# A hybrid encoder layer: two-block chunks in the opening, up rows a pair ahead, the down stage's memory in order of release, and the last norm with its products beside it

## The chip, the cores and the metric

The kernel runs on one core of one Trainium2 chip. The metric is the time of one execution on the device in microseconds. Before the change it is 1643.92 us, the median of three runs (1643.7 to 1643.96). A core has five engines with queues of their own, worked off in order: TensorE (PE in the profile; its weight loads are PEld), VectorE (DVE), ScalarE (ACT), GpSimd (POOL) and SyncE (SP, which here only issues transfers).

## The reference

One layer over 1024 prompt frames and 8 times 16 sample frames, 1152 rows of 1024 columns together:

```python
h = rmsnorm(x, g_pre_mix)
qa, ka, va, qb, kb, vb, ga, gb = project(h, w_in)          # one product, 1024 -> 4352 columns
oa = band_attention(qa, ka, va, bias_a, sink)              # own chunk and 2 before, 8 heads on 2
ob = band_attention(qb, kb, vb, bias_b, None)              # own chunk and 8 before, 8 heads
merged = sigmoid(ga) * (oa @ w_oa) + sigmoid(gb) * (ob @ w_ob)
x = x + rmsnorm(merged @ w_out, g_post_mix)
u, g = split(rmsnorm(x, g_pre_ffn) @ w_upg)                # 1024 -> 2 x 3072
c = conv_b + sum over tap of conv_w[tap] * upad[:, tap:tap + s]   # causal, width 3
x = x + rmsnorm((gelu(c) * g) @ w_down, g_post_ffn)
```

`rmsnorm(x, g)` is x divided by the root of its mean square over a row (plus 1e-6), times g. The new keys, values and convolution rows are returned too.

## The kernel before, in words

All products run on TensorE with factors split into a high and a low part, so that one product of a block is three matmuls (high by high, and the two mixed ones; `chunk_product`, L143). The big products (projection, up, down) use a scheme of Strassen and Winograd: the factors are cut in two by two quarters, seven products of quarters replace eight, and sums and differences of quarters (the forms) are made on VectorE and ScalarE beforehand. The rows are the columns of the right factor: half of the 1152, 576, go through two PSUM banks as two chunks of 288 columns (`CW`).

*Opening.* Nine blocks of 128 rows of x are fetched by SyncE. Class `Block` squares a block on ScalarE with a sum per row (L274), gets the root from VectorE (L96) and GpSimd (L97), multiplies by root and gain on VectorE (`norm`, L278), transposes it on TensorE (L286, eight transposes into two banks `tp`), and writes the high part on ScalarE (L302) and the low part on VectorE (L307) into the right factor `xk`. The gain is a row that one transfer spreads over 128 partitions (L79). Class `Away` (L222) holds the products of the first quarter alone for seven pairs of output tiles (`ixh`), which need no forms. They fill TensorE while the blocks come in: `run` makes twelve matmuls of one half and one chunk, `copy` brings the result from PSUM to `ia0h` or `ia1h` on ScalarE. The order of TensorE, ScalarE and VectorE in the opening is written out by hand (L316 on). Beside it run the position tables: a product `pe` (L392), a copy `ea`, and the store of `tab_a`.

*Projection.* `right_factors` makes the forms (`sums`, L408, and their high and low parts, L208 and L209, named `t`). For each pair of tiles, `head` and `tail` (L440, L456) run the products: first `iz` and `ix` with the forms, and last `iz` with `a_i`. `left_factors` makes forms of the weight tiles (L127 to L133) and splits them (L173, L174). `plus` adds a PSUM bank to a tile (L188).

*Up stage.* 24 pairs of tiles of the up weights; a tail multiplies, `take` copies PSUM out, then follow the convolution (L1195, L1197, L1199), the gate, and four stores of the result to DRAM (`z_dr`, L1217 to L1223). For the first pairs (`NH` = 5), part of the convolution's rows was put to DRAM earlier and comes back by three transfers (L1204, `w<-c_dr`). The tile `w` that they land in alternates between two (`r1[f % 2]`). After the last pair, the new convolution rows are stored (L1259).

*Down stage.* `raws` (L1288 on) fetches pairs of z tiles and down weights (names such as `z12r`, `wd12r`: one transfer for each of the two tiles, L1295 and L1296), `split` and `split_samples` make high and low parts, and TensorE multiplies into `p20s` and others (L1366), which are gathered in `yacc`. The tiles of this stage take the memory of the up stage's; where a tile lies decides which earlier instruction it must wait for, and with it the order in which SyncE's queue is filled. `finish` (L1404) makes the last norm of a block of rows: a square on ScalarE, scaling and power on GpSimd, then on VectorE the product with root and gain (L1419) and the sum with the residual (L1422), and the store. `start_finish` runs it in two steps, so that the second step of one block lies behind the products of the next.

Outside of the manual stretches a scheduler sets the order of each engine's instructions.

## Time and profile before

| | us |
|---|---|
| median of three runs | 1643.92 |
| profiled execution, its own time | 1648.29 |
| profiled execution, span | 1646.5 |
| TensorE busy | 1591.7 |
| VectorE busy | 1096.0 |
| ScalarE busy | 726.1 |
| GpSimd busy | 215.9 |
| mean granted clock of TensorE | 0.992 of full |

The span is the time between the first and the last recorded instruction; the execution's own time holds a little more around it. Busy time is the sum over the whole span; it does not say whether an engine's idle time matters. That is read from the waits: an idle stretch ends when something else has finished, and the profile names that something behind an arrow. A granted clock of 1.00 is TensorE's level of 2.4 GHz, 0.50 that of 1.2 GHz, and a value between them is a mixture within the stretch.

### The profile page before, as it was taken

Reading aid. Unit: us, or ns where it says so; the run is one execution under the profiler, and the core shown is the slowest. Engines: PE = TensorE matmul, PEld = TensorE weight load, DVE = VectorE, ACT = ScalarE, POOL = GpSimd, SP = SyncE. Lnnn points to the kernel's source line nnn. Section 1 sums busy time; section 2 is a strip of 40 time slices with the busy share of each in tenths; the row PEclk is TensorE's granted clock in tenths of the full one; section 3 lists DMA queues with packets and bytes.
Section 4 is the critical chain, followed back from the end, with each engine's and each line's share of the span. In section 5 each row is a group of like instructions: output and inputs, shape, how many; then the busy total and the mean of one; then the engine's idle time right before and its main releaser. Section 6 shows DMA issues by size and latency. Waiting matters only on the chain. (4 is left out here: it accounts for less than half of the span.)

```text
span 1646.5 us, 27860 instructions
## 1 busy us (share of the span) xinstructions
PE 1591.7 (97%) x10887; PEld 1471.5 (89%) x10887; DVE 1096.0 (67%) x2015; ACT 726.1 (44%) x1411; POOL 215.9 (13%) x293
## 2 busy tenths in 40 slices
PE   6999999999999999999999999999999998999997
PEld 5999999878788889978799999999999997888886
DVE  6965544677777746353597866667666665966986
ACT  7611233566555544332373344444444444534342
POOL 1000000221110004310002311122111110000004
PEclk9999999999999999999999999999999999999999
DMA  7743321664543155342164312212212228053023
GB/s 257 250 166 136 119 95 73 215 183 146 167 152 102 60 198 183 120 166 90 67 205 139 106 66 81 69 67 81 81 66 81 75 80 314 1 215 110 1 100 130
DMA packets 93636, 206.47 MB, mean 125 GB/s; under 512 B 19464, under 2 KB 43320, under 8 KB 93504
## 3 DMA queue, kind: packets, MB, share of 16 engines
q1 hardware_dynamic: 93504, 204.69, 36.4%
q8 instruction: 85, 1.39, 0.3%
q14 instruction: 47, 0.39, 0.1%
HBM read 148.13 MB, written 61.24 MB: 127 GB/s over the span
## 5 line engine op out<-in xcount | busy, mean ns | idle before, releaser
L143 PE MATMUL x<-xot,s 128*128 128x288 f32 x1152 | 157.7, 295 | 1.5 <-DVE w L1156 1.5
L143 PEld LDWEIGHTS x<-xot,s 128*128 128x128 f32 x1152 | 154.9, 188 | 1.7 <-ACT a L1019 1.7
L1366 PE MATMUL x<-wbp,zap 128*128 128x512 f32 x576 | 135.3, 389 | 0.0
L1366 PEld LDWEIGHTS x<-wbp,zap 128*128 128x128 f32 x576 | 108.1, 188 | 22.5
L1366 PE MATMUL p<-wbp,zap 128*128 128x512 f32 x432 | 102.4, 394 | 0.0
L1019 ACT ACTIVATE s<-uw 128x512 fp32r<-128x512 f32 x96 | 60.1, 627 | 94.6 <-issue 42.0
L671 ACT ACTIVATE p<-p,m 128x256 f32<-128x256 f32 (+4 forms) x128 | 74.8, 586 | 56.5 <-DVE m L666 56.5
L1366 PEld LDWEIGHTS p<-wbp,zap 128*128 128x128 f32 x432 | 82.4, 191 | 17.3
L1020 DVE TENSOR_TENSOR s<-uw,s 128x512 fp32r<-128x512 f32 x96 | 70.1, 730 | 34.0 <-ACT s L1019 34.0
L1197 DVE SCALAR_TENSOR_TENSOR wk<-w,cw,wk 128x128 f32<-128x128 f32 (+2 forms) x144 | 83.2, 614 | 7.4 <-ACT wk L1195 6.6
L1020 DVE TENSOR_TENSOR a<-uw,a 128x512 fp32r<-128x512 f32 x62 | 42.9, 693 | 63.3 <-ACT a L1019 62.0
L143 PE MATMUL x<-xob,s 128*128 128x288 f32 x576 | 81.1, 295 | 3.2 <-ACT wk L1195 1.4
L143 PEld LDWEIGHTS x<-xob,s 128*128 128x128 f32 x576 | 78.1, 188 | 3.8 <-ACT wk L1195 1.6
L143 PE MATMUL z<-xot,s 128*128 128x288 f32 x576 | 80.7, 295 | 0.0
L143 PE MATMUL z<-xot,a 128*128 128x288 f32 x576 | 80.7, 295 | 0.0
L143 PE MATMUL ix<-t,s_i 128*128 128x288 f32 x576 | 78.6, 295 | 0.3 <-DVE iu L188 0.3
L143 PEld LDWEIGHTS z<-xot,s 128*128 128x128 f32 x576 | 78.1, 188 | 0.0
L143 PEld LDWEIGHTS z<-xot,a 128*128 128x128 f32 x576 | 78.1, 188 | 0.0
L143 PEld LDWEIGHTS ix<-t,s_i 128*128 128x128 f32 x576 | 77.2, 188 | 0.5 <-issue 0.5
L173 ACT ACTIVATE s_i<-iw 128x512 fp32r<-128x512 f32 x48 | 30.3, 630 | 88.4 <-PE ix L143 49.0
L143 PE MATMUL x<-xob,a 128*128 128x288 f32 x456 | 63.9, 295 | 0.0
L143 PE MATMUL y<-xob,a 128*128 128x288 f32 x456 | 63.9, 295 | 0.0
(625 smaller groups left out, 3828.2 us busy)
## 6 DMA issues: line engine op xcount, KB each, us to landing
uw<-in_w_upg SPq DMA_DIRECT2D x53, 512.0 KB, 4.4
iw<-in_w_in SPq DMA_DIRECT2D x31, 512.0 KB, 4.6
gg<-in_dr SPq DMA_DIRECT2D x16, 576.0 KB, 3.7
z_dr<-wk SPq DMA_DIRECT2D x24, 256.0 KB, 2.1
in_dr<-gt SPq DMA_DIRECT2D x30, 192.0 KB, 1.9
z_dr<-wk SPq DMA_DIRECT2D x24, 224.0 KB, 1.9
xt<-in_x SPq DMA_DIRECT2D x9, 512.0 KB, 10.1
oT<-o_dr SPq DMA_DIRECT2D x8, 576.0 KB, 5.3
```

The source lines that it names most:

```text
L143: nc.tensor.matmul(ps, w[:, i, k], right(j, c, k), start=first and n == 0, stop=last and n == len(todo) - 1, skip_group_check=True)
L173: nc.scalar.activation(sp[:, 0], src, AF.Copy)
L671: nc.scalar.activation(p[h][:, 0:n], p[h][:, 0:n], AF.Exp, bias=least[h], scale=-1.0, accum_out=st.d[:, h, i:i + 1])
L1019: nc.scalar.activation(sp[:, 0], src, AF.Copy)
L1020: nc.vector.tensor_tensor(sp[:, 1], src, fr(sp[:, 0]), op=ALU.subtract)
L1197: nc.vector.scalar_tensor_tensor(out, src(t), cw[:, f, t:t + 1], out, op0=ALU.mult, op1=ALU.add)
L1366: nc.tensor.matmul(ps, z[:, i, k, c], w[:, j, k], start=first and n == 0, stop=last and n == 2, skip_group_check=True)
```

## The change

In the projection, the two chunks of 576 columns are 256 and 320 wide instead of 288 and 288, so that the first chunk of the first products is two blocks of rows. The gain of the first norm comes as one row of 4 KB on ScalarE's queue and is spread over the partitions by two matmuls with a column of ones; the first two blocks read it from PSUM, the others from a copy. The rows of weights for `Away` are packed two to a buffer. The up rows of a pair are asked for during the pair before. In the down stage the order of the memory pools changes, the stores of the last pair and of the convolution rows move to GpSimd's queue, and the gain of the last norm is fetched later. In the last norm the product with the gain is made apart, in halves and beside the square; the scaling is on VectorE; root and residual are applied in one instruction.

```diff
+    widths = (2 * P, 2 * CW - 2 * P)
     def chunk(c):
-        return slice(c * CW, (c + 1) * CW)
+        return slice(c * widths[0], widths[0] + c * widths[1])
...
+        def away_weights(f):
+            if f not in wraws:
+                box = wraw.tile([P, 2, KD, P], F32, name=f"iwh{f}", tag="uw")
+                for i in range(2 - (f + 1 == NA)):
+                    nc.sync.dma_start(box[:, i], w_in[pairs[f + i][0]])
+                    wraws[f + i] = box[:, i]
+            return wraws[f]
...
+            g1 = xs.tile([1, D], F32, name="g1")
+            nc.scalar.dma_start(g1[:], g_pre_mix[None, :])
+            ones = xs.tile([1, P], F32, name="ones")
+            nc.vector.memset(ones[:], 1.0)
+            gps = [psx.tile([P, 512], F32, name=f"gps{i}", tag="ps") for i in range(2)]
+            for i in range(2):
+                nc.tensor.matmul(gps[i][:], ones[:], g1[:, i * 512:(i + 1) * 512], start=True, stop=True)
+            gp = xs.tile([P, D], F32, name="gp")
...
-                if tb == 0:
-                    gp = bcast_row(xs, g_pre_mix, D, "gp")
...
                 def norm(self):
+                    if self.tb < 2:
+                        for i in range(2):
+                            c = slice(i * 512, (i + 1) * 512)
+                            nc.vector.scalar_tensor_tensor(self.xn[:, c], xts[self.tb][:, c], self.st[:, 1:2], gps[i][:],
+                                                           op0=ALU.mult, op1=ALU.mult)
+                        return
...
+        def up_rows(f):
+            if f not in got:
+                w = r1[f % 2].tile([P, 4 * 3 * 256], F32, name=f"w{f}", tag="act")
...
+                if f < NH:
+                    for dst, c, cols, samples in rows(u, us):
+                        nc.sync.dma_start(dst, by_sample(c_dr[f][:, c, cols], samples))
+                got[f] = w, u, us
+            return got[f]
...
-            w = r1[f % 2].tile([P, 4 * 3 * 256], F32, name=f"w{f}", tag="act")
+            w, u, us = up_rows(f)
+            if f + 1 < NH:
+                up_rows(f + 1)
...
-            nc.sync.dma_start(z_dr[f][:, H1:512], c2[:, 0:512 - H1])
+            queue = nc.gpsimd if f == NF - 1 else nc.sync
+            queue.dma_start(z_dr[f][:, H1:512], c2[:, 0:512 - H1])
...
-        nc.sync.dma_start(conv_new, cnew)
+        nc.gpsimd.dma_start(conv_new, cnew)
...
-        for q in range(3):
-            zp[q], wp[q] = right(f"zp{q}"), right(f"wp{q}")
+        def split_pools(q):
             za.append(right(f"za{q}"))
             wb.append(right(f"wb{q}"))
-            if q == 0:
-                yacc = right("yacc").tile([P, NT, 2, 512], F32, name="yacc")
+        split_pools(0)
+        zp[0], wp[0] = right("zp0"), right("wp0")
+        split_pools(1)
+        for q in (1, 2):
+            zp[q], wp[q] = right(f"zp{q}"), right(f"wp{q}")
+        split_pools(2)
         zsp = [right(f"zs{i}") for i in range(6)]
         for q in range(3, 6):
             zp[q], wp[q] = right(f"zp{q}"), right(f"wp{q}")
+        yacc = right("yacc").tile([P, NT, 2, 512], F32, name="yacc")
...
-            rstd_of(st[:, 0:1], st[:, 2:3], nc.gpsimd)
+            last = n == NT - 1
+            for i in range(2):
+                c = slice(i * 512, (i + 1) * 512)
+                if i:
+                    yield
+                    nc.vector.tensor_scalar(st[:, 0:1], st[:, 0:1], 1.0 / D, EPS, op0=ALU.mult, op1=ALU.add)
+                nc.vector.tensor_tensor(yg[:, c], yt[:, c], gpo[:, c], op=ALU.mult)
+                sq = bank(psv, f"sq{tb}{i}")
+                nc.scalar.activation(sq, yt[:, c], AF.Square, accum_out=st[:, i:i + 1])
+            nc.vector.tensor_scalar(st[:, 2:3], st[:, 1:2], 1.0 / D, st[:, 0:1], op0=ALU.mult, op1=ALU.add)
+            nc.gpsimd.tensor_tensor(st[:, 2:3], st[:, 2:3], nhalf[:, 0:1], op=ALU.pow)
             yield
...
+            for c in [slice(0, 512), slice(512, D)] if last else [slice(0, D)]:
+                nc.vector.scalar_tensor_tensor(yt[:, c], yg[:, c], st[:, 2:3], x1[:, c], op0=ALU.mult, op1=ALU.add)
                 nc.sync.dma_start(y[tb][:, c], yt[:, c])
...
+        def start_finish(tb, products, add):
+            ends = finish(tb, box["n"])
+            next(ends)
             box["n"] += 1
+            products()
+            if box["n"] == NT:
+                next(pending.pop(), None)
+            add()
             next(ends)
```

TensorE's queue at the start of the program, before: `tp` are a block's transposes, `ixh_0` and `ixh_1` the two chunks of an `Away` product, `xk_128` and `xk_129` its two halves.

```order
L286 MATMUL tp_0_200<-ident,xn_190 128x128 x4
L286 MATMUL tp_1_205<-ident,xn_190 128x128 x4
L286 MATMUL tp_0_228<-ident,xn_196 128x128 x4
L286 MATMUL tp_1_233<-ident,xn_196 128x128 x4
L286 MATMUL tp_0_248<-ident,xn_224 128x128 x4
L286 MATMUL tp_1_253<-ident,xn_224 128x128 x4
L143 MATMUL ixh_0_268<-xk_128,ih_0_215 128x288 x12
L286 MATMUL tp_0_281<-ident,xn_244 128x128 x4
L286 MATMUL tp_1_286<-ident,xn_244 128x128 x4
L143 MATMUL ixh_0_268<-xk_129,ih_0_218 128x288 x12
```

The same place after the change (`gps` are the products that spread the gain):

```order
L274 MATMUL gps_167<-g_163,ones 128x512
L274 MATMUL gps_168<-g_163,ones 128x512
L314 MATMUL tp_0_207<-ident,xn_196 128x128 x4
L314 MATMUL tp_1_212<-ident,xn_196 128x128 x4
L314 MATMUL tp_0_233<-ident,xn_203 128x128 x4
L314 MATMUL tp_1_238<-ident,xn_203 128x128 x4
L143 MATMUL ixh_0_252<-xk_128,ih_0_225 128x256 x12
L314 MATMUL tp_0_280<-ident,xn_248 128x128 x4
L314 MATMUL tp_1_285<-ident,xn_248 128x128 x4
L143 MATMUL ixh_0_252<-xk_129,ih_0_228 128x256 x12
L143 MATMUL ixh_0_313<-xk_128,ih_1_267 128x256 x12
```

The first twelve matmuls stand behind the transposes of two blocks instead of three, and two products of the gain stand ahead of all.

VectorE's queue after the change, from the low parts of the last `Away` weights on; the first `sums` is the row that writes where the position tables' tiles lay.

```order
L177 TENSOR_TENSOR ih_4_692<-iwh_689,ih_4_692 128x512
L212 TENSOR_TENSOR xk_128<-b_148,xk_128 128x4x256
L212 TENSOR_TENSOR xk_128<-b_148,xk_128 128x4x320
L177 TENSOR_TENSOR ih_4_695<-iwh_689,ih_4_695 128x512
L438 TENSOR_TENSOR sums<-b_149,b_148 128x4x256
L438 TENSOR_TENSOR sums<-b_149,b_148 128x4x320
L212 TENSOR_TENSOR t_615<-sums,t_615 128x4x256
L177 TENSOR_TENSOR ih_5_756<-iwh_689,ih_5_756 128x512
```

The low parts of `xk` stand ahead of the first form now; all that follows stands behind it.

SyncE's queue at the start of the down stage, before:

```order
L1223 DMA z_dr_9204<-wk 128x128
L1475 DMA gpo<-in_g_post_ffn 128x1024
L1295 DMA z14r<-z_dr_9196 128x1152
L1296 DMA wd14r<-in_w_down 128x1024
L1295 DMA z14r<-z_dr_9197 128x1152
L1295 DMA z12r<-z_dr_9194 128x1152
L1296 DMA wd12r<-in_w_down 128x1024
L1295 DMA z12r<-z_dr_9195 128x1152
L1259 DMA out<-st 128x432
L1296 DMA wd12r<-in_w_down 128x1024
L1296 DMA wd14r<-in_w_down 128x1024
L1222 DMA z_dr_9205<-wk 128x448
```

After:

```order
L1266 DMA z_dr_9212<-wk 128x128
L1344 DMA z12r<-z_dr_9202 128x1152
L1345 DMA wd12r<-in_w_down 128x1024
L1344 DMA z12r<-z_dr_9203 128x1152
L1345 DMA wd12r<-in_w_down 128x1024
L1344 DMA z14r<-z_dr_9204 128x1152
L1345 DMA wd14r<-in_w_down 128x1024
L1344 DMA z14r<-z_dr_9205 128x1152
L1345 DMA wd14r<-in_w_down 128x1024
L1344 DMA z16r<-z_dr_9206 128x1152
```

The first pair's loads stand ahead of the second's and together, and the store of the convolution rows (`out<-st`) and the last pair's stores of z have left the queue.

## Rows read from the trace of the kernel before

**Rows 1.** The page, busy time, share of the span and instructions
```profile
PE 1591.7 (97%) x10887; PEld 1471.5 (89%) x10887; DVE 1096.0 (67%) x2015; ACT 726.1 (44%) x1411; POOL 215.9 (13%) x293
```

**Rows 2.** Table of waits, TensorE: waiter, releaser, us in total, times, longest
```profile
PE tp L286 <- DVE xn L278: 12.9, 5, 7.9
PE p20s L1366 <- ACT wbp L1304: 5.8, 1, 5.8
...
PE x L143 <- DVE w L1156: 1.5, 1, 1.5
...
PE x L143 <- DVE wk L1156: 0.5, 1, 0.5
```

**Rows 3.** Timeline, TensorE, opening: start us, length us, instruction, idle before
```profile
39.14 1.06 PE L286 MATMUL tp<-ident,xn 128*128 128x128 f32 x8 [0.18 <-DVE xn L278]
...
46.36 0.81 PE L392 MATMUL pe<-oh,tt 32*8 32x384 f32 x2
...
52.28 24.38 PE L143 MATMUL ixh<-xk,ih 128*128 128x288 f32 x168 [1.74 <-ACT ia0h L239]
76.50 3.34 PE L143 MATMUL iz<-t,s_i 128*128 128x288 f32 x24
79.68 3.35 PE L143 MATMUL ix<-t,s_i 128*128 128x288 f32 x24
```

**Rows 4.** Timeline, VectorE, opening
```profile
6.58 1.28 DVE L278 SCALAR_TENSOR_TENSOR xn<-xt,st,gp 128x1024 f32<-128x1024 f32 x1 [0.83 <-DMA gp<-in_g_pre_mix]
...
34.58 1.35 DVE L408 TENSOR_TENSOR sums<-b,b 128x1152 f32<-128x1152 f32 x1
35.85 0.15 DVE L96 TENSOR_SCALAR st<-st 128x1 f32<-128x1 f32 x1
...
74.66 1.29 DVE L174 TENSOR_TENSOR s_i<-iw,s_i 128x512 fp32r<-128x512 f32 x2
```

**Rows 5.** Timeline, ScalarE, opening
```profile
49.37 0.63 ACT L173 ACTIVATE ih<-iw 128x512 fp32r<-128x512 f32 x1 [2.25 <-DMA iw<-in_w_in]
```

**Rows 6.** The page, transfers: count, KB each, median us to landing
```profile
z_dr<-wk SPq DMA_DIRECT2D x24, 224.0 KB, 1.9
```

**Rows 7.** Timeline, SyncE's queue, start of the down stage
```profile
1363.77 0.34 SPq L1259 DMA_DIRECT2D out<-st  x1
1364.15 0.43 SPq L1296 DMA_DIRECT2D wd12r<-in_w_down  x1
```

**Rows 8.** Timeline, ScalarE, start of the down stage
```profile
1370.95 1.06 ACT L1304 ACTIVATE wbp<-wd12r 128x1024 fp32r<-128x1024 f32 x1 [2.22 <-DMA wd12r<-in_w_down]
```

**Rows 9.** Timeline, TensorE, start of the down stage
```profile
1372.06 0.80 PE L1366 MATMUL p20s<-wbp,zs 128*128 128x512 f32 x1 [5.82 <-ACT wbp L1304]
...
1381.31 0.84 PE L1366 MATMUL p20s<-wbp,zs 128*128 128x512 f32 x3
...
1394.91 0.84 PE L1366 MATMUL p10s<-wbp,zs 128*128 128x512 f32 x3
```

**Rows 10.** Windows: us, busy (count) by engine, granted clock, DMA share, GB/s
```profile
1372.00:1374.00 2.00, 1.94 (x5) 1.56 (x6) 1.96 (x2) 1.07 (x2) 0.00 (x0) 0.50 0.94 235
```

**Rows 11.** Timeline, all engines, end
```profile
1636.12 0.69 DVE L1378 TENSOR_TENSOR yacc<-yacc,x 128x512 f32<-128x512 f32 x1 [0.94 <-PE x L1366]
...
1636.84 0.63 ACT L1413 ACTIVATE sqf<-yacc 128x512 f32<-128x512 f32 x1 [2.16 <-DVE yacc L1378]
...
1638.14 1.17 POOL L96 TENSOR_SCALAR stf<-stf 128x1 f32<-128x1 f32 x1
...
1639.98 1.42 DVE L1419 SCALAR_TENSOR_TENSOR yacc<-yacc,stf,gpo 128x512 f32<-128x512 f32 x2 [0.72 <-POOL stf L97]
...
1641.43 1.63 DVE L1422 TENSOR_TENSOR yacc<-yacc,x1f 128x512 f32<-128x512 f32 x1
```

**Rows 12.** Groups: busy us, mean ns of one, idle before
```profile
L143 PEld LDWEIGHTS x<-xot,s 128*128 128x128 f32 x1152 | 154.9, 188 | 1.7 <-ACT a L1019 1.7
...
L720 PE MATMUL o<-pk,vs 128*64 128x256 f32 x192 | 24.3, 388 | 0.0
```

More of the change, by code (lines that the diff above doesn't have):

```diff
@@ L148, in product, with banks @@
             chunk_product(ps[c], w, right, c, first, last)
-    def banks(pool, name):
-        return [pool.tile([P, 512], F32, name=f"{name}_{c}", tag="ps")[:, 0:CW] for c in range(2)]
+    def banks(pool, name, widths=(CW, CW)):
+        return [pool.tile([P, 512], F32, name=f"{name}_{c}", tag="ps")[:, 0:n] for c, n in enumerate(widths)]
+    widths = (2 * P, 2 * CW - 2 * P)
     def chunk(c):
-        return slice(c * CW, (c + 1) * CW)
+        return slice(c * widths[0], widths[0] + c * widths[1])
     xkp = xk_stack.enter_context(tc.tile_pool(name="xk", bufs=1, reuse_waits="tile"))
@@ L187, in plus @@
             for c in range(2):
-                nc.vector.tensor_tensor(out[:, c], ps[c], t[:, c], op=ALU.add)
+                nc.vector.tensor_tensor(out[:, chunk(c)], ps[c], t[:, chunk(c)], op=ALU.add)
             return out
         def store(t, tile_no, half):
-            nc.sync.dma_start(in_dr[tile_no][:, half * 2 * CW:(half + 1) * 2 * CW], t[:].rearrange("p c n -> p (c n)"))
+            nc.sync.dma_start(in_dr[tile_no][:, half * 2 * CW:(half + 1) * 2 * CW], t[:])
         pairs = [(4, 5), (0, 1), (2, 3), (10, 14), (6, 7), (11, 15)] + [(18 + n, 26 + n) for n in range(6)]
         NA = 7
-        a1_dr = [dram.tile([P, 2, CW], F32, name=f"a1_dr{f}") for f in range(NA)]
+        a1_dr = [dram.tile([P, 2 * CW], F32, name=f"a1_dr{f}") for f in range(NA)]
         rf = {}
@@ L209, in parts_of, with weights @@
             nc.vector.tensor_tensor(lo, src, fr(hi), op=ALU.subtract)
-        def weights(f, n=2):
-            raw = wraw.tile([P, 2, KD, P], F32, name=f"iw{f}{n}", tag="uw")
-            for i in range(n):
+        def weights(f):
+            raw = wraw.tile([P, 2, KD, P], F32, name=f"iw{f}", tag="uw")
+            for i in range(2):
                 nc.sync.dma_start(raw[:, i], w_in[pairs[f][i]])
             return raw
+        def away_weights(f):
[5 more added lines that the diff above has]
+            return wraws[f]
         for i, name in enumerate(("b11", "b12")):
@@ L226, in __init__ @@
                 self.f, self.pool, self.early = f, pool, early
-                raw = wraws.pop(f, None) or weights(f, 1)
-                self.left = [split_left(raw[:, 0, 4 * i:4 * i + 4], f"ih1{i}_{f}") for i in range(2)]
+                raw = away_weights(f)
+                self.left = [split_left(raw[:, 4 * i:4 * i + 4], f"ih1{i}_{f}") for i in range(2)]
                 self.out = [two_chunks(f"ia{i}h{f}") for i in range(2)]
@@ L259, in encoder_step @@
                 xts.append(xt)
-                if tb == 0:
-                    gp = bcast_row(xs, g_pre_mix, D, "gp")
+                if tb == 1:
+                    box = wraw.tile([P, 2, KD, P], F32, name="iwh0", tag="uw")
                 if tb in (1, 3):
-                    wraws[tb // 2] = weights(tb // 2, 1)
+                    wraws[tb // 2] = box[:, tb // 2]
+                    nc.sync.dma_start(wraws[tb // 2], w_in[pairs[tb // 2][0]])
             class Block:
@@ L320, in encoder_step @@
                 b[0].transposed()
+                for i in range(2):
+                    nc.scalar.activation(gp[:, i * 512:(i + 1) * 512], gps[i][:], AF.Copy)
+                b[1].norm()
                 b[0].high()
-                b[1].norm()
                 b[0].low()
                 w0 = Away(0, psx, True)
-                enter()
                 b[1].transposed()
                 b[1].high()
+                b[1].low()
+                enter()
+                w0.run(0, 0)
                 b[2].norm()
-                b[1].low()
+                w0.copy(0, 0)
+                w1 = Away(1, psx, True)
                 enter()
@@ L453, in head_back @@
             nc.sync.dma_start(a[:], a1_dr[f][:])
-            return left_factors(weights(f), True, f"i{f}", split_left), banks(psx, f"ix{f}"), a
+            return left_factors(weights(f), True, f"i{f}", split_left), banks(psx, f"ix{f}", widths), a
         def tail(f, ops, xb, a, forms):
@@ L461, in tail @@
             t0, t1 = pairs[f]
-            zb = banks(psz, f"iz{f}")
+            zb = banks(psz, f"iz{f}", widths)
             product(zb, next(ops), of(rf["t3"]), True, False)
@@ L1200, in conv @@
                 return c
-            for dst, c, cols, samples in rows(u, us):
-                if yb is None:
-                    nc.sync.dma_start(dst, by_sample(c_dr[f][:, c, cols], samples))
-                else:
+            if yb is not None:
+                for dst, c, cols, samples in rows(u, us):
                     nc.vector.tensor_tensor(dst, by_sample(yb[c][:, cols], samples), by_sample(a[c][:, cols], samples),
```

83 lines of the change are left out of this document (33 added, 50 removed).

## The prediction, made before the changed kernel was run

> **What bounds the kernel now.** I read the busy line of the page first: TensorE is busy for 1591.7 us [rows 1] of a span of 1646.5, so the time is TensorE's work plus 54.8 us in which it has none. The table of TensorE's waits then says which of those gaps this change can reach [rows 2]: 12.9 us of transposes that wait for the first norms, 5.8 us at the start of the down stage, and four short waits of the up stage from 1.5 to 0.5 us (4.6 us together). The timelines of the engines in those places give the rest: what ended each wait, and what TensorE lost beside it. Behind the last products, which end just before the last add at 1636.12, comes a chain of small instructions on four engines [rows 11], and any microsecond taken from it counts in full. Elsewhere TensorE is dense, and only the pace of its matmuls could change anything.
>
> All sums are made against the profiled execution (1648.29 us, span 1646.5). The median of the runs shown is 1643.92, 4.4 us lower; I take the same difference from it.
>
> **Opening.** Three things change. The first norm no longer waits for a 512 KB broadcast of the gain (0.83 us idle ahead of it [rows 4]), which also stood ahead of the second block of x on SyncE's queue; the two one-row products that replace it need 4 KB and run before TensorE has anything else. The first product needs two blocks, not three. And weight rows two to five are asked for earlier. I walked the new orders of the engines with the durations of the trace: the transposes of the last block, at 39.14 before [rows 3], come out near 38.35, since blocks two to eight still cost one square, one power and one norm each. By then half a run of twelve matmuls more is done (0.7 us), so 1.5 us are gained there. Then the wait of 1.74 us ahead of 52.28 goes [rows 3]: ScalarE had waited 2.25 us for a weight row, until 49.37 [rows 5], and its copies that free TensorE's banks were queued behind. From 52.28 to 76.50 the 168 matmuls take 24.22 us, where at full clock 24 take 3.18 (76.50 to 79.68), 22.26 for 168 [rows 3]; the 1.96 us between is a lower clock after that wait, and goes with it. Together 1.5 + 1.74 + 1.96 = 5.2 us: the first tail starts near 71.3.
>
> What is late next is VectorE. In the new order nearly all of the Winograd forms stand behind one instruction, the first that writes the sums. Its memory is that of the position table's tiles, so it waits for the store of that table; before, the first form ran at 34.58 [rows 4]. The table's product, at 46.36 before [rows 3], comes 1.5 us earlier with the products around it: 44.9. Its own 0.8 us, ScalarE's copy of 0.5, which no longer stands behind a wait, and some 2.3 for issue and landing (1.9 us for a small store [rows 6]) make 48.5. Behind it on VectorE stand, up to the left factor of the tail's last product, twenty pieces of the forms' sums and low halves, at 256 or 320 columns and 1.27 us on average (34.58 to 35.85), thirteen 512-column steps of 0.60 us (two in 1.29, pipelined) [rows 4], and eight pieces of a quarter of that size, some 0.4 us by my estimate from these: 25.4 + 7.8 + 3.2 = 36.4 us. With 1 us for releases that is 85.9. TensorE, starting at 71.3, wants the factor four products of 3.2 us later, at 84.1, and I count 0.2 us more for an earlier piece. So about 2.0 us go back, while 0.3 us of a wait that the same place had before comes off: net 5.2 − 2.0 + 0.3 = 3.5 us. The two ends: 7.0 us if the forms aren't late and the earlier blocks gain more, and 1.0 us if the first form only starts at 51.
>
> **Chunk widths.** 2016 matmuls of the projection go from 288 columns to 1008 of 256 and 1008 of 320. At 288 one takes 3.18 / 24 = 132.5 ns [rows 3]; at 512, sixty take 13.60 us from 1381.31 to 1394.91, 226.7 ns each [rows 9]. The line through both is 0.42 ns a column, which gives 119.0 and 145.9, in sum 265 as before: nothing. From above, 256 columns cost the 126.6 ns of the attention's products of that shape (24.3 us over 192) [rows 12], 7.6 ns more than the line, 7.7 us lost over 1008; from below, the 132.5 ns scaled by columns (117.8) gives 1.2 us gained. The attention's products wait on copies between them, so I take the line: zero.
>
> **Up rows.** The code asks for the up rows one pair ahead, but the tile that they land in is one that the pair before last releases, and the new order of SyncE's queue has the fetches at the same places, behind the same stores. I price it at nothing, and expect the four waits [rows 2] again.
>
> **Start of the down stage.** Before, SyncE's queue held the store of the convolution state until 1363.77, and the second half of the first down weights only left behind it, at 1364.15 [rows 7]. ScalarE waited 2.22 us for that load until 1370.95 [rows 8], and TensorE 5.82 us, until 1372.06 [rows 9]. Then the clock: the 90 products from 1372.06 to 1394.91 took 22.85 us where six rounds of 3.40 are 20.40 [rows 9], so 2.45 us more, with a granted clock of 0.50 at first, the level of 1.2 GHz [rows 10]. Now the loads of the first pair lead the queue and the stores stand on GpSimd's. What the first load needs is memory that the last heads release before the stage; the four loads of the first pair, 2.2 MB, then have time to land. I take 5.82 + 2.45 = 8.27, less 0.4 for a first copy that still comes late: 7.9 us. The other end is 3, if a z tile of the first pairs comes as late as the last head allows.
>
> The new waits: copies into the output accumulator, on ScalarE and VectorE, now stand behind the stores of the last pair, which lie on its memory, and a later weight load behind the state's store. These copies come some 20 us into the stage. If such a store takes as long as the slowest load of this place (1364.15 to 1370.95, 6.8 us [rows 7, 8]), 10 us of cover are left; if the cover is gone, every microsecond counts, since products need the banks that these copies free. No transfer of before left GpSimd's queue, so its own landing time is not shown. The Trainium skill (SBUF — State Buffer, "SBUF: two separate sides") speaks against that queue: the descriptors of its transfers are written by GpSimd, and VectorE can lock it out while certain operations run; no row here shows it. By that rule the stores land late, and the sum would stay at 7.9 us up to a delay of 10 us, and lose one for one beyond it.
>
> **The end.** Before: the last add at 1636.12 (0.69), the square at 1636.84 (0.63) and its read, GpSimd's sum and its scaling at 1638.14 (1.17), its power, VectorE's two products from 1639.98 and its last add until 1643.06 [rows 11]. Now the scaling is one VectorE instruction (0.15 us as in the opening [rows 4]), and product and add are one instruction for each half, on a product made beside the square. The last add is held by the block before's final instruction, which is put ahead of it, by my walk until 1636.75. Then: add to 1637.45, square and read to 1638.3, scaling to 1638.5, power to 1639.1, two halves of 0.75 to 1640.6. That is 2.5 us gained; 3.2 if the add isn't held; 1.0 if the pieces wait on one another.
>
> **Sum.** 3.5 + 0 + 0 + 7.9 + 2.5 = 13.9 us: the profiled execution would be 1634.4, the median 1643.92 − 13.9 = 1630.0.
>
> **Rivals.** *VectorE eats the opening's gain*: the first form at 51 or later. For it speaks the long list behind that form; against it, that ScalarE's wait ahead of the table's copy goes. Opening 0, total 10.4: 1633.5. *The opening gives all*: the store lands early enough; opening 7.0, total 17.4: 1626.5. Against it stands the table's product, which TensorE still runs at its place among the others. *The down stage still waits*: its first loads are queued in front of one that waits for the last head, and 3 us come back; total 9.0: 1634.9. *The up rows do act*: 4.6 us more, 1625.4; the queue's unchanged order speaks against it, and then that part of the change would do what its code says.
>
> On the other side, *the 256-column matmul is paced by its weight load*: a load's record is 188 ns long beside every matmul [rows 12]. If at 256 columns it no longer fits, 1008 of them at 188 − 119 = 69 ns are 69 us lost: 1699. It decides from 13.9 us / 1008 = 13.8 ns on, 132.8 ns for a matmul of 256. Against it: at 288 columns matmuls follow each other every 132.5 ns with loads of that record, so the record is not the pace, and the attention's 256 run at 126.6.
>
> **How the numbers follow.** Forecast 0.54; opening eaten 0.19; opening all 0.11; down stage still waits 0.08; up rows act 0.03; weight-load pace 0.05. The forecast's own range is 1628 to 1632. All cases but the last two lie between 1626.5 and 1634.9; with part of the bound on the widths the range is 1625.5 to 1636. A measurement of this kernel tells 0.2%, 3.3 us, from no change. All cases but the last are faster by more than twice that; a part of the last (from 10.6 us of loss on) is no change, most of it slower: faster 0.94, same 0.02, slower 0.04.
>
> **What would show it.** In the changed kernel's timeline: the last block's transposes near 38.3; no wait near 50, the clock at full from 50 to 60; VectorE idle until about 48.5 ahead of its first sums, and TensorE waiting some 2 us for a left factor between 77 and 87; the four up-stage waits unchanged; the first product of the down stage within 0.5 us of the last of the up stage, at the level of 2.4 GHz; VectorE's scaling of 0.15 us and an end 4.5 us behind TensorE's last matmul. The forecast is wrong if 256 and 320 columns differ in sum from 265 ns, or if the loads of the down stage collide with the stores of the last pairs.

## The result, and the profile after

The changed kernel takes 1631.77 us (median of four runs, 1631.33 to 1635.94) against 1643.94 for the kernel before; the ratio is 0.9928, with a 95% interval from 0.9909 to 0.9947. The forecast was 1630.0, and the time lies 0.2 us inside the end of the forecast's own range (1628 to 1632). Six more runs of the changed kernel (e9 below) have a median of 1633.07, beside 1645.54 for the kernel before: the gain repeats, 12.2 and 12.5 us. Its profiled execution took 1635.94 us, with a span of 1634.1, against 1648.29 and 1646.5: 12.4 us less in both measures, where the sum had 13.9.

Where they came from is seen by cutting both traces at the same instructions of TensorE and comparing the lengths. The boundaries are the starts of: the first `iz` product, the end of the projection (its last product), the first transpose `pt` and the first product `mp`, the first `xh`, the last product of the up stage, the first `p20s`, the first `p10s`, then the end of the last matmul and of the span. The last column is a second trace of the changed kernel, from the experiments. Each column is one execution; what other traces of the same code have in these stretches is told with the experiments, and it matters for the opening and for the start of the down stage.

| stretch, us | before | changed | gained | changed again |
|---|---|---|---|---|
| opening, to the first tail | 76.50 | 71.89 | 4.61 | 72.35 |
| projection | 223.39 | 224.23 | −0.84 | 223.30 |
| on to the attentions | 8.12 | 8.25 | −0.13 | 8.68 |
| attentions | 295.72 | 296.81 | −1.09 | 297.75 |
| gates, output, norms | 215.34 | 216.14 | −0.80 | 214.22 |
| up stage | 546.88 | 547.27 | −0.39 | 547.13 |
| last up product to first down product | 6.11 | 0.13 | 5.98 | 0.13 |
| first six rounds of the down stage | 22.85 | 20.45 | 2.40 | 20.45 |
| rest of the down stage | 241.17 | 241.14 | 0.03 | 241.18 |
| behind TensorE's last matmul | 10.41 | 7.78 | 2.63 | 7.77 |

The opening on TensorE in the changed kernel (columns as in the timelines before):

```profile
36.52 1.06 PE L314 MATMUL tp<-ident,xn 128*128 128x128 f32 x8 [0.57 <-ACT ih L176]
...
68.61 3.44 PE L143 MATMUL ixh<-xk,ih 128*128 128x256 f32 x24 [2.24 <-ACT ia0h L251]
71.89 3.33 PE L143 MATMUL iz<-t,s_i 128*128 128x256 f32 x24
...
86.32 2.91 PE L143 MATMUL iz<-t,a_i 128*128 128x256 f32 x20 [0.92 <-DVE a_i L177]
...
97.65 2.03 PE L143 MATMUL ix<-t,s_i 128*128 128x320 f32 x12 [0.66 <-DVE iu L191]
```

The last transposes come at 36.52 instead of 39.14, and the wait at 52.28 of [rows 3] is gone. But a new one of 2.24 us, for the same kind of copy, stands at 68.61, and two of 0.92 and 0.66 us in the tails (in the second trace 1.48 us at 69.07, 0.90 in the tails, and nothing for the last). Behind the first of these stand VectorE, ScalarE and SyncE's queue, in this order:

```profile
47.62 2.63 DVE L438 TENSOR_TENSOR sums<-b,b 128x1024 f32<-128x1024 f32 x2 [1.61 <-DMA tab_a<-ea]
...
63.75 0.69 DVE L127 TENSOR_TENSOR iw<-iw 128x512 f32<-128x512 f32 x1 [2.35 <-DMA iw<-in_w_in]
```

```profile
67.01 1.27 ACT L211 ACTIVATE t<-sums 128x1280 fp32r<-128x1280 f32 x1 [1.53 <-DVE sums L438]
68.19 0.69 ACT L251 ACTIVATE ia0h<-ixh 128x256 f32<-128x256 f32 x2
```

```profile
47.51 4.96 SPq L92 DMA_DIRECT2D ext_a<-tab_a  x8
...
54.18 0.32 SPq L255 DMA_DIRECT2D a_dr<-ia0h  x1
54.59 1.70 SPq L217 DMA_DIRECT2D iw<-in_w_in  x2
```

VectorE's first `sums` waits for the table's store until 47.62 (34.58 in [rows 4]). Later VectorE stands 2.35 us, until 63.75, for the first pair of whole weights, whose load left at 54.59: behind eight transfers of the table that held SyncE's queue for 5 us, and directly behind a store of `Away` results that waits for ScalarE's copy. ScalarE's copy of a form waits for the `sums` behind it, and the copies `ia0h`, which free TensorE's banks, stand behind that one.

The start of the down stage, on TensorE and on SyncE's queue:

```profile
1364.72 0.87 PE L1415 MATMUL p20s<-wbp,zs 128*128 128x512 f32 x3
...
1385.17 0.84 PE L1415 MATMUL p10s<-wbp,zs 128*128 128x512 f32 x3
```

```profile
1348.01 0.40 SPq L1344 DMA_DIRECT2D z12r<-z_dr  x1
...
1350.49 0.43 SPq L1345 DMA_DIRECT2D wd12r<-in_w_down  x1
```

The loads of the first pair leave together, the second half of the weights at 1350.49, where [rows 7] has it at 1364.15. The first product follows the last head with no wait, and the 90 products take 20.45 us, the full clock's pace, against 22.85 in [rows 9]. The first copy into the accumulator, on ScalarE, and the largest store of the last pair, now on GpSimd's queue (the fence of transfers gives KB and us to landing):

```profile
1382.70 0.60 ACT L1425 ACTIVATE yacc<-p20s 128x512 f32<-128x512 f32 x1 [0.74 <-PE p20s L1415]
```

```profile
z_dr<-wk POOLq DMA_DIRECT2D x1, 256.0 KB, 6.1
```

The copy is released by its product, not by the stores: the last of them landed by 1376, over 6 us earlier. The end, all engines:

```profile
1625.80 1.28 DVE L1474 SCALAR_TENSOR_TENSOR yacc<-ygf,stf,x1f 128x1024 f32<-128x1024 f32 x1
1627.00 0.68 DVE L1427 TENSOR_TENSOR yacc<-yacc,x 128x512 f32<-128x512 f32 x1
...
1628.47 0.21 DVE L1470 TENSOR_SCALAR stf<-stf 128x1 f32<-128x1 f32 x1
...
1629.41 1.42 DVE L1474 SCALAR_TENSOR_TENSOR yacc<-ygf,stf,x1f 128x512 f32<-128x512 f32 x2 [0.73 <-POOL stf L1471]
```

The last add stands behind the block before's final instruction, which begins at 1625.80, and starts at 1627.00; VectorE's scaling takes 0.21 us where GpSimd's took 1.17 [rows 11]. The four waits of the up stage are still there, 4.8 us in all (4.7 before):

```profile
PE x L143 <- DVE wk L1200: 3.3, 3, 1.4
PE x L143 <- DVE w L1200: 1.5, 1, 1.5
```

### The profile page after: what moved, and what is told of

The parts are those of the page before. It is cut to its first block, busy times and chain, and to the rows that moved or that the text cites. A ratio compares the mean times of both kernels' runs of the same rounds, so it can differ in the third digit from the quotient of the medians.

```text
span 1634.1 us, 27922 instructions
## 1 busy us (share of the span) xinstructions
PE 1593.4 (98%) x10891; PEld 1470.7 (90%) x10891; DVE 1099.4 (67%) x2045; ACT 728.7 (45%) x1429; POOL 212.1 (13%) x287
## 4 chain that ended last, share of the span: by engine, by line
PE 86%; DVE 5%; ACT 3%; DMA 3%; issue 2%; POOL 1%; SPq 0%; DVEq 0%; POOLq 0%; ACTq 0%
PE x L143 16%; PE z L143 8%; PE x L1415 8%; PE ix L143 7%; PE p L1415 6%; PE iz L143 4%; PE y L143 4%; PE o L750 2%; PE d L117 2%; PE pt L735 2%; PE d L119 2%; PE r L1090 2%; PE mp L956 2%; PE mp L958 2%; PE mp L957 2%; PE d L118 2%
## 5 line engine op out<-in xcount | busy, mean ns | idle before, releaser
L143 PE MATMUL ix<-t,s_i 128*128 128x256 f32 (+1 forms) x576 | 78.4, 294 | 0.7 <-DVE iu L191 0.7
```

The costliest lines, as they stand in the source:

```text
L143: nc.tensor.matmul(ps, w[:, i, k], right(j, c, k), start=first and n == 0, stop=last and n == len(todo) - 1, skip_group_check=True)
```

## The experiments

Ten kernels were run. Their times scatter by some 3 us about the median between executions of one program, in part for the reason that run e9 shows, so where a stage is asked for, its length in the trace decides.

**The gain's row elsewhere (e1).** The forms were late because the opening's pool had grown by 4.6 KB a partition, and the sums came to lie on the table's tiles. Here the two new tiles go to other pools:

```diff
-            g1 = xs.tile([1, D], F32, name="g1")
+            g1 = wop.tile([1, D], F32, name="g1", tag="wop")
...
-            ones = xs.tile([1, P], F32, name="ones")
+            ones = pa.tile([1, P], F32, name="ones", tag="a")
```

> The changed kernel, with the gain's row and the column of ones put into the pools of the weight parts and copies, so that the opening's own pool is as small as in the kernel before and the forms' sums no longer lie on the position table's tiles. Theory 1 (VectorE's forms are late because of that overlap, and TensorE's waits of 2.24 us at 68.6, 0.92 at 86.3 and 0.66 at 97.7 come from it): the first form near 34, all three waits gone, 3.0 to 3.8 us less than the changed kernel's 1631.8, about 1628.3. Rival (the first pair of whole weights lands late at 63.7 whatever VectorE does, and holds it): the waits stay within 1 us, no more than 1 us gained.

Measured: 1633.54 us (1632.30 to 1635.36, six runs), ratio to before 0.9933 (0.9916 to 0.9950). VectorE and TensorE in its trace:

```profile
35.55 1.22 DVE L438 TENSOR_TENSOR sums<-b,xk 128x1024 f32<-128x1024 f32 x1
...
64.19 0.69 DVE L127 TENSOR_TENSOR iw<-iw 128x512 f32<-128x512 f32 x1 [2.84 <-DMA iw<-in_w_in]
```

```profile
38.65 1.07 PE L314 MATMUL tp<-ident,xn 128*128 128x128 f32 x8 [0.99 <-DVE xn L306]
...
68.87 3.44 PE L143 MATMUL ixh<-xk,ih 128*128 128x256 f32 x24 [1.67 <-ACT ia0h L251]
...
78.93 3.74 PE L143 MATMUL ix<-t,s_i 128*128 128x256 f32 x24 [0.28 <-DVE iu L191]
```

The first sums run at 34.35, as expected, and the second, shown here, at 35.55. Three traces have the changed kernel's opening unaltered: its own, that of e9 and that of e8. All three have a wait of 0.90 to 0.92 us for a left factor in the first tail, and it is gone here; one of 0.28 us stands at another place. The projection takes 222.83 us, against 224.23, 223.30 and 223.29 in the three. But the wait at 68 stays: 1.67 us here and 1.76 in e10, which has the same edit, against 2.24, 1.48 and 1.24; and VectorE still stands for the weights until 64.19. So theory 1 holds for the tails and the rival for the first wait. The last transposes, too, are later (38.65), since two forms now run ahead of the last norm on VectorE. Net, from the start to the end of the projection, 294.97 against 296.12, 295.65 and 295.70: 0.7 to 1.2 us, not 3 or more, and nothing that shows in the median.

**The sums in another slot (e2).** The order of VectorE's queue stays, only what the first form waits for changes:

```diff
-        tpool = [ph.enter_context(tc.tile_pool(name=f"t{i}", bufs=1, reuse_waits="tile")) for i in (3, 2, 1, 4)]
+        t3p, t2p, t4p, t1p = [ph.enter_context(tc.tile_pool(name=f"t{i}", bufs=1, reuse_waits="tile")) for i in (3, 2, 4, 1)]
+        tpool = [t3p, t2p, t1p, t4p]
```

> The changed kernel with the memory of the sums and of one form exchanged: the first form still stands at the same place of VectorE's queue but waits for the table's product and not for the store of the table. Theory 1a (the wait of 1.6 us for the store is what costs): the first form at 46.0 instead of 47.6, and 1.6 us of TensorE's 3.8 us of waits gone, 1630.2. Theory 1b (it is the place in the order, behind the low parts of four other pieces, that costs, not the wait): less than 0.7 us gained, 1631.1 to 1632.

Measured: 1632.36 us (1629.98 to 1637.97, six runs), ratio 0.9929 (0.9908 to 0.9949).

```profile
46.32 2.62 DVE L439 TENSOR_TENSOR sums<-b,b 128x1024 f32<-128x1024 f32 x2
50.55 1.23 DVE L212 TENSOR_TENSOR t<-sums,t 128x1024 fp32r<-128x1024 f32 x1 [1.61 <-ACT t L211]
```

```profile
67.95 3.44 PE L143 MATMUL ixh<-xk,ih 128*128 128x256 f32 x24 [1.17 <-ACT ia0h L251]
...
85.66 2.91 PE L143 MATMUL iz<-t,a_i 128*128 128x256 f32 x20 [0.90 <-DVE a_i L177]
```

The first form starts at 46.32, without a wait. But VectorE's next instruction, a low part, now stands 1.61 us for ScalarE's copy of the same form and starts at 50.55, where the changed kernel has it at 50.16. So the wait was not taken away, it moved one instruction on: had the store come earlier in the changed kernel, VectorE would have stood for that copy instead. TensorE's wait at 68 is 1.17 us, which the scatter of the same opening reaches (1.24 in e8), the 0.92 stays 0.90, and the projection ends 0.3 to 0.7 us earlier than in the three traces. That speaks for 1b: the wait for the store costs nothing by itself, since ScalarE's copies, in their own order, hold the list as well.

**The table's rows on GpSimd's queue (e7).** On top of e1, to free SyncE's queue ahead of the weights:

```diff
-            replicate(tab_a, ext_a, ea, EXT_A)
+            replicate(tab_a, ext_a, ea, EXT_A, nc.gpsimd)
```

> The kernel of the run with the gain's row elsewhere, and besides the eight transfers that spread the position table (192 KB each) on GpSimd's queue instead of SyncE's. Theory 4 (TensorE's wait of 1.67 us at 68.9, which stayed, comes from the first whole weights, whose load is issued behind those eight, 5 us of SyncE's queue): the load issued near 53.4 instead of 55.4, landed near 62, and TensorE's wait under 0.5 us, the first tail at 70.5 instead of 72.15. Rival (that the eight transfers share the DMA engines with the load is what costs, whichever queue issues them): the load lands at 63.5 or later, the wait stays over 1 us.

Measured: one run, 1635.23 us.

```profile
63.20 0.69 DVE L127 TENSOR_TENSOR iw<-iw 128x512 f32<-128x512 f32 x1 [2.15 <-DMA iw<-in_w_in]
```

```profile
71.44 3.33 PE L143 MATMUL iz<-t,s_i 128*128 128x256 f32 x24
...
79.34 3.74 PE L143 MATMUL ix<-t,s_i 128*128 128x256 f32 x24 [1.40 <-DVE iu L191]
```

VectorE has its weights at 63.20 instead of 64.19, and the wait of 1.67 us is gone: the first tail starts at 71.44. The queue was one cause, as theory 4 says. The load landed 1.2 us later than expected, but the blocks of this execution came 1.1 us later than e1's too (the last transposes at 39.74 instead of 38.65). Nothing shows of it at the end: TensorE, earlier by 0.7 us, now waits 1.40 us at 79.34 for VectorE, and the projection ends at 295.38, after e1's 294.97. One run with later blocks does not tell whether a part of the gain would stay.

**The widths alone (e3).** The kernel before, with the first lines of the change's diff (256 and 320 columns) and nothing else.

> The kernel before with the chunk widths 256 and 320 alone. Theory (a matmul's time follows its columns; the two traces show the projection's products 0.7 us shorter over its length): the projection 0.5 to 1.2 us shorter, total 1642.7 to 1643.5. Rival of the prediction (256 columns paced by the weight load): up to 69 us longer, from 1 us on seen in the projection's length. Rival by the attention's 256-column products: 7.7 us longer.

Measured: 1644.55 us (1640.25 to 1648.23, twelve runs) against 1644.28; ratio 0.9999 (0.9986 to 1.0012). The projection takes 222.38 us instead of 223.39. 0.1 us of this is a shorter wait; the rest, 0.9 us or 0.4%, is the pace of the matmuls (0.8 to 1.0 us in all by the other traces of before's projection, 223.1 to 223.4). In the time itself it does not show, the interval being wider than that. From one start to the next, 256 columns take 117.9 ns in this trace and 320 take 146.7, where 288 took 132.8 before. The rival of the weight load falls. The line through 288 and 512 columns was 1.1 ns too high for 256 and 0.8 too low for 320, and the two errors nearly cancel in the sum.

**The memory order alone, and the queues alone (e4, e6).** The first has the change's new order of pools, with all stores on SyncE's queue; the second has the stores on GpSimd's queue and the memory as before.

> The kernel before with the down stage's memory order alone; all stores stay on SyncE's queue. Theory 2 (the first pair's loads come early because of the memory they lie on): most of the 8.4 us at the start of the down stage, 1635.5 to 1637.5. Rival (the store of the convolution rows in SyncE's queue, which waits for GpSimd's last copy, is what holds the loads, so the memory alone gives little): under 3 us gained, above 1641.

> The kernel before with the last pair's stores and the convolution rows' store on GpSimd's queue alone, the memory order as before. Theory 2: with the memory as before the first pair's loads still wait for the last head's release, so TensorE's gap ahead of the first product of the down stage stays over 3 us of the 5.8. Rival (the store in SyncE's queue was what held the second half of the weights): the gap under 2 us.

Measured: e4 1637.39 us (1636.18 to 1642.88, seven runs), ratio 0.9961 (0.9943 to 0.9978); e6, one run, 1648.43 (before, beside it, 1645.19). TensorE at the start of the down stage, e4 first and then e6, and SyncE's queue of e6:

```profile
1362.49 0.87 PE L1372 MATMUL p20s<-wbp,zs 128*128 128x512 f32 x3
...
1382.96 0.84 PE L1372 MATMUL p10s<-wbp,zs 128*128 128x512 f32 x3
```

```profile
1370.22 0.50 PE L1367 MATMUL p20s<-wbp,zs 128*128 128x512 f32 x1 [2.37 <-ACT wbp L1305]
...
1373.15 1.22 PE L1367 MATMUL p20s<-wbp,zs 128*128 128x512 f32 x2 [1.52 <-DVE wbp L1306]
```

```profile
1355.08 0.32 SPq L1296 DMA_DIRECT2D z14r<-z_dr  x1
...
1359.97 0.32 SPq L1296 DMA_DIRECT2D z12r<-z_dr  x1
```

With the memory order alone the gap is 0.13 us and the six rounds take 20.47, 20.60 together: all of the 8.4 us by the trace of before. With the queues alone the waits are 2.37 and 1.52 us, and the rounds take 24.89 us because the clock falls as before. The first wait lies between the 3 us of theory 2 and the 2 of its rival. Gap and rounds together take 27.56 us, 1.4 less than before's 28.96; but e3 and e5, whose code at this place is before's, have 27.03 and 27.10, so the queues alone gain nothing that can be told, and the memory order gains 6.4 to 8.4 us. The first loads of e6 leave at 1355.08 and 1359.97, each when the tile beneath it is released. Theory 2 is shown by e4; the store of the convolution rows was only the last of the waits in that queue: without it the second half of the first weights leaves 4 us earlier against the last product of the up stage, and TensorE still waits.

**The last norm alone (e5).** The kernel before with the change's `finish` and `start_finish`.

> The kernel before with the new last norm alone. Theory 3 (the end becomes shorter because GpSimd's scaling of 1.17 us, its sum and the separate last add go): from TensorE's last matmul to the end 7.8 us instead of 10.4, the 2.6 us that the two traces differ by; the start of the down stage as before. Rival (a part of those 2.6 us comes from the loads and stores that the new memory order moved): under 1.5 us.

Measured: one run, 1641.48 us (before, beside it, 1645.19). Behind TensorE's last matmul it needs 7.83 us (before 10.41, changed 7.78), so all of the 2.6 us are the norm's. Its end:

```profile
1634.97 1.41 DVE L1425 SCALAR_TENSOR_TENSOR yacc<-ygf,stf,x1f 128x512 f32<-128x512 f32 x2 [0.73 <-POOL stf L1422]
```

The start of the down stage was expected as before, and its code is. In this execution TensorE waits there for 3.02 us, where [rows 9] has 5.82:

```profile
1366.92 0.80 PE L1366 MATMUL p20s<-wbp,zs 128*128 128x512 f32 x1 [3.02 <-ACT wbp L1304]
```

The same load of weights took 6.7 us to land in the trace of before, 5.6 in that of e3 and 3.9 here, and gap and six rounds together take 28.96, 27.03 and 27.10 us. So one trace of before is not the measure of this place.

**The up rows in a tile of their own (e8).** The prefetch now has a place to land that is free a pair earlier, for pairs 2 and 4:

```diff
-                u = w[:, 0:UT]
+                u = w[:, 0:UT] if f not in (2, 4) else work["st"][:, NF * 34:NF * 34 + UT]
```

> The changed kernel with the up rows of pairs 2 and 4 in a part of another tile that is free, so that asking for them a pair ahead can act; pair 3 keeps its place. Theory 5 (the prefetch does nothing since the tile is released too late): the waits of TensorE near 882 and 918 (1.4 and 0.5 us before) go, the one near 900 stays: 1.5 to 2.0 us less between the first product of the up stage and its last. Rival (those waits come from VectorE's or ScalarE's own lag): less than 0.5 us.

Measured: one run, 1631.05 us. TensorE's waits in the changed kernel, and then in this one:

```profile
882.32 3.43 PE L143 MATMUL x<-xob,s 128*128 128x288 f32 x24 [1.43 <-DVE wk L1200]
...
899.79 3.43 PE L143 MATMUL x<-xob,s 128*128 128x288 f32 x24 [1.24 <-DVE wk L1200]
...
918.23 1.86 PE L143 MATMUL x<-xob,s 128*128 128x288 f32 x12 [0.61 <-DVE wk L1200]
```

```profile
857.49 3.43 PE L143 MATMUL x<-xot,s 128*128 128x288 f32 x24 [0.91 <-DVE w L1200]
...
875.93 1.84 PE L143 MATMUL x<-xot,s 128*128 128x288 f32 x12 [0.61 <-DVE w L1200]
...
895.02 3.42 PE L143 MATMUL x<-xob,s 128*128 128x288 f32 x24 [1.10 <-DVE wk L1200]
...
909.95 1.86 PE L143 MATMUL x<-xot,s 128*128 128x288 f32 x12 [0.31 <-DVE w L1200]
```

Pair 3 keeps its wait (1.24, now 1.10). Those of pairs 2 and 4, for `wk`, are gone; shorter ones for another tile (0.61, 0.31) stand near them. The up stage is 1.4 us shorter (545.84 against 547.27), a little less than the 1.5 to 2.0 expected, and 0.6 us of it stand at a wait that the edit does not touch (0.91 at 857.49, 1.52 in the changed kernel, 0.90 in e2). In e10, with the same edit, the waits of pairs 2 and 4 for `wk` are gone too. The prefetch of the change did nothing because of the tile, as theory 5 has it; what it is worth with a free tile is some 1 us.

**The changed kernel again (e9).**

> The changed kernel once more, for a second trace of the same program. Theory 6 (the 2.3 us that the profiled execution lost between the projection and the up stage come from stretches of 3.4 or 6.8 us at half the granted clock, which fall differently in each execution): the end of the projection, the start of the down stage behind the last head, and the end within 0.3 us of the first trace's lengths, while the half-clock stretches near 420, 600 and 706 are others in number or length, and the attention's length differs by 1 us or more. Rival (the change itself slows the attention, through memory or queues): the same stretches and the same lengths again, within 0.3 us.

Measured: 1633.07 us (1630.79 to 1635.34, six runs), ratio to before on that chip 0.9919 (0.9905 to 0.9934). Two windows, in the attentions and behind them, in the trace of before, of the changed kernel and of its second trace (columns as in [rows 10]; the granted clock stands third from the right):

```profile
415.00:430.00 15.00, 12.00 (x97) 9.93 (x98) 12.11 (x36) 8.35 (x24) 3.40 (x5) 1.00 0.60 194
598.00:612.00 14.00, 11.21 (x54) 10.57 (x54) 6.48 (x5) 8.13 (x8) 0.00 (x0) 0.88 0.95 338
```

```profile
415.00:430.00 15.00, 12.02 (x100) 9.20 (x101) 9.86 (x32) 7.22 (x22) 0.85 (x1) 0.89 0.53 184
598.00:612.00 14.00, 11.38 (x50) 11.06 (x49) 6.48 (x5) 10.43 (x10) 0.00 (x0) 0.76 0.97 368
```

```profile
415.00:430.00 15.00, 12.09 (x70) 9.13 (x69) 9.13 (x31) 6.96 (x21) 0.59 (x1) 0.77 0.48 166
598.00:612.00 14.00, 11.38 (x57) 11.05 (x56) 6.48 (x5) 9.97 (x10) 0.00 (x0) 0.88 0.96 370
```

TensorE's busy time in these windows is alike (12.0 to 12.1 and 11.2 to 11.4 us), and so are its longest idle spells (2.42, 2.39 and 2.41 us in the first, 2.62 in the second of all three), and the granted clock differs: 1.00 and 0.88 before, 0.89 and 0.76 in the changed kernel, 0.77 and 0.88 in its second trace. At half the clock 0.89 over 15 us is some 3.3 us, and 0.77 is 6.9. The attentions take 295.72, 296.81 and 297.75 us, and what follows 215.34, 216.14 and 214.22. The stages behind them repeat within 0.2 us; the opening, the projection and the step behind it do not (0.4 to 0.9), which the expectation had not allowed for. The lengths of the attentions and of the stage after move by 0.9 and 1.9 us between two traces of one program, as much as between before and after (for the attentions 1 us or more was expected).

All twelve traces, of before's code and of the changed one, can be set side by side in these two stages, which no edit touches. Gates, output and norms take 213.0 to 213.9 us in the six traces that have 3.4 us at half clock there, 214.1 to 214.2 in the four with 6.6 to 6.8 us, 215.3 with 10.2 (before) and 216.1 with 13.0 (the changed kernel): there theory 6 holds, and the rival falls. The attentions take 295.7 to 299.6 us in five traces of before's code and 295.5 to 298.6 in seven of the changed one, so the change does not slow them; but the clock explains their scatter only in part, since with 3.4 us at half clock they take anything from 295.5 to 298.2.

**Both extras together (e10).** The edits of e1 and e8.

> The changed kernel with the gain's row elsewhere and the up rows of pairs 2 and 4 in a tile of their own, together. The two act in different stages: 1.2 us from the first (by its trace), 1.6 us from the second, so 2.8 us less than the changed kernel on the same chip, between 1628 and 1630. Rival (they share a resource, or the half-clock stretches decide): less than 1 us in the median.

Measured: 1631.65 us (1630.44 to 1636.39, six runs), 1.4 us under the changed kernel's 1633.07 on the same chip, ratio to before 0.9918 (0.9903 to 0.9932). The expectation had 2.8 us and 1628 to 1630, the rival less than 1 us: neither came. The intervals overlap, so it is not told from the changed kernel. In its trace the half clock fell into the opening as well, behind the wait that e1 had left:

```profile
70.04 4.96 PE L143 MATMUL ixh<-xk,ih 128*128 128x256 f32 x24 [1.76 <-ACT ia0h L251]
```

These 24 products take 4.96 us, where e1 has them in 3.44.

## Why the prediction was right, and where it was not

*Opening.* Forecast: the first tail near 71.3; it starts at 71.89 (72.35 and 72.41 in e9 and e8, whose opening is the same). Steps were off on both sides and cancel, so the nearness is in part luck. The last transposes come at 36.5, 37.7 and 38.0 in these three traces, not at 38.35: I carried over the pace of the blocks of before, though the earlier weights and blocks shorten it. The step "then the wait of 1.74 us ahead of 52.28 goes" holds only for its place: a wait of 2.24 us for the same copies comes back at 68.61, and of 1.48 in e9:

```profile
69.07 3.45 PE L143 MATMUL ixh<-xk,ih 128*128 128x256 f32 x24 [1.48 <-ACT ia0h L251]
```

And the 1.96 us of lower clock "after that wait" belong to one execution. Three more traces have before's opening, instruction by instruction: those of e4, e5 and e6. The same wait stands in them, 1.51, 1.10 and 0.75 us, but the clock stays at full behind it, as in e4's:

```profile
52.51 22.57 PE L143 MATMUL ixh<-xk,ih 128*128 128x288 f32 x168 [1.51 <-ACT ia0h L239]
```

The 168 matmuls take 22.57 us where [rows 3] has 24.38, and the first tail starts at 74.91, 74.79 and 73.71 instead of 76.50. So the term for the clock was a gain against that one trace, not against the kernel.

I had VectorE's lateness reach TensorE only through the factors of the tail. It also reaches it through ScalarE, whose copies of forms wait for VectorE and hold the copies that free the banks; and the first whole weights, whose place in SyncE's queue I had not looked at, hold VectorE itself. The first form at 48.5 was measured at 47.62, 48.94 and 48.91, but by e2 the store that it waits for is not what makes the forms late. Its price in the tails was 0.92 + 0.66 = 1.58 us, and 0.9 in the other two traces, where I had 2.0. Net, at the first attention, 3.65 us (3.5 forecast, with the widths' 0) between the two traces; by the means of the four traces of before's opening and the three of the changed one it is 2.1.

*Widths.* Forecast zero; 0.9 us gained by e3: 117.9 and 146.7 ns for 256 and 320 columns, 264.6 in sum against two of 132.8. The bound from above, the attention's products, was no measure, and the rival of the weight load did not come. The bound from below was none: it scaled 256 by its columns and left 320 on the line; scaled as well, 320 would take 147.2 ns and the sum would stay at 265.

*Up rows.* As forecast, and e8 shows the reason given.

*Down stage.* 5.98 + 2.40 = 8.38 us against 7.9; the 0.4 I had set aside for a late first copy was not needed. e4 gives all of it to the memory order. But 5.82 and 2.45 us, too, were read off one execution, whose load of weights was slow; against e3 and e5 the gain is 6.4 us, so 7.9 was near the upper end of what the order is worth. Of GpSimd's queue the Trainium skill (SBUF — State Buffer, "SBUF: two separate sides") says that its transfers can be held up while VectorE runs certain operations. The last pair's two large stores took 6.1 and 6.3 us to land, where the same ones on SyncE's queue take a median of 2.1 and 1.9; in e4, with the same memory order, the smaller of the two left SyncE's queue at about this place and took 2.2. The transfers beside it ran at 288 GB/s there and at 414 here, so whether the queue or the loads did it is not separated, and no run shows VectorE's part in it. The cover held with over 6 us to spare.

*End.* 2.63 us against 2.5, by the steps given: the add at 1627.00 is 0.7 us behind the last matmul, as the walk had it.

*What the sum left out.* It has 13.9, the two traces 12.4, the medians 12.2. In the traces the terms named come to 3.65 + 5.98 + 2.40 + 2.63 = 14.7. The rest, 1.09 + 0.80 + 0.39 = 2.3 us, was lost in stages that no term touches: the first two by the scatter that e9 shows, the 0.39 of the up stage within the scatter there (546.2 to 547.3 us over seven traces without a half clock in it). The forecast had TensorE's clock only where a wait of the change stands. So what failed is the premise of the sum, "I take the same difference from it": the trace of before was 4.4 us slower than the median, and part of that excess stood in the very waits that were priced, the half clock in the opening and the slow load at the start of the down stage. The change could take that away from the one trace, but not in full from the median. The means of the traces with the same code, three or four of each, give 2.1 us for the opening and projection, 7.1 for the start of the down stage and 2.6 for the end, 11.8 in sum and near the 12.2 of the medians. That the 14.7 of the two traces came down to 12.4 is chance: in the stages that the change does not touch, the changed kernel's trace happened to be the longer one.

## What to carry to other kernels

Before a tile is added to a pool, see whose memory lies behind it: 4.6 KB for a row and ones moved all forms 13 us back, and an order of pools alone gave 6.4 to 8.4 us at a stage's start. A load asked for earlier only comes earlier if the tile that it lands in is free. A wait that is taken away in a full list can come back one instruction later, as in e2, or on another engine, as in e7. And before a wait is priced from one trace, see in a second trace of the same program whether it has the same length: of the 5.2 us summed for the opening here, 1.96 had no counterpart in three other traces.

## What the runs showed of the hardware

TensorE's granted clock fell to half for a stretch within or shortly behind the same few idle spells, of 1.7 to 2.8 us (2.4 to 5.8 at the start of the down stage with before's memory order), but not at each of them in every trace, nor for as long: near 420 us, behind idle spells of 2.4 us, not at all in the trace of before, for some 3.3 us in the changed kernel, 6.9 in its second trace; in the opening, behind 1.74 us, in the trace of before, and not in that of e4 behind 1.51 or of the changed kernel behind 2.24. A part of the scatter of the times goes with it: of six executions of the changed kernel, the two at a mean clock of 0.997 took 1630.8 and 1630.9 us, the one at 0.993 1635.3. One load of 512 KB, issued at the same place of the same code, took 6.7, 5.6 and 3.9 us to land in three traces. Matmuls of 256, 288 and 320 columns followed each other every 117.9, 132.8 and 146.7 ns, so that products at 256 and 320 together were 0.4% faster than two at 288.
